# Two of the six modulation rows of a feed-forward are summed on VectorE instead of TensorE

## Chip, core and metric

The program runs on one core of one Trainium2 chip. The metric is device time in microseconds (us) of one execution, given as the median of several runs. TensorE, VectorE (DVE), ScalarE (ACT), GpSimd (POOL) and the DMA queue of SyncE (SP) work side by side; each has its own list of instructions and takes them in that order.

## The reference, cut to what matters

Two blocks follow each other on 256 tokens of width 1024. The first (gated convolution, mLSTM, mixture of experts) is not touched. The second has two layers; all of it is float32:

```python
cond = silu(c)                                        # one row of 1024
for i in range(2):
    mod = (cond @ ada_w[i] + ada_b[i])[:, None, :]    # ada_w[i] is 1024 x 6144
    shift1, scale1, gate1, shift2, scale2, gate2 = split(mod, 6, axis=-1)
    h = rmsnorm(x, norm1_g[i]) * (1.0 + scale1) + shift1
    x = x + gate1 * attention_i(h)
    h = rmsnorm(x, norm2_g[i]) * (1.0 + scale2) + shift2
    x = x + gate2 * swiglu(h, f_w_in[i], f_w_out[i])
```

The change concerns `shift2` and `scale2` of layer 0 of this second block: a vector of 1024 against a matrix of 1024 x 1024, twice.

## The kernel before, in words

Large products are made from float32 operands split in a high and a low part (`split`, lines 92 to 109: ACT copies the high part, DVE subtracts it for the low part) and three matmuls for each pair (`mm3`, line 127). Weights come in pieces of 1 MB into eight buffers named `raw` (`load`, line 74), each load being one instruction in SP's list that waits until a buffer is free.

The modulation rows (`ada_steps`, line 187) are matmuls of a different kind: the conditioning column, repeated to 32 columns, is the stationary operand, and 512 columns of `ada_w` move. Four such matmuls go to four column groups of the array (output partitions 0, 32, 64, 96) into one PSUM bank. A step is one load of 1 MB and four matmuls; the bias is added by further matmuls of the same output shape from a 12-row tile (`bias`). The last step copies the bank out (`adarow`), and either turns it into columns (`ada_cols`, tile `adac`) or spreads it over all partitions (`ada_gate`, tile `adag`).

The steps are not run where they are needed. They stand in a Python list, `queue`, and `fill` (line 182) takes the next one at fixed places: after each of the twelve weight pieces of attention 0 (`dense`, steps "D"; tile `dense`), after each of its eight heads (`values`, steps "V") and after each piece of the feed-forward's first product (`first`; tiles `fg` and `fu`). Attention 0 so has 20 places. Before the change the list for layer 0 has 19 entries: `ada1` (gate1 and shift2, 8 loads and an end), `ada2` (scale2, 4 loads and an end), `ada3` (gate2, 4 loads and an end). The 9 entries of the next layer's `ada0` follow when feed-forward 0 begins. The list's order is the program's order; the framework then sets each engine's own order from it, so that steps move a little to either side.

In attention 0 the string at line 1287 is the order of the work. After three weight pieces come the transposes of queries and keys (`pT`, copied out by ACT into `T`), the scores of two heads (`sc`), softmax on DVE and ACT (`nm`, `ee`), then for each head four transposes of the weights (`wT`), a copy by ACT (`wTs`) and four matmuls with the values (`po`), then scores of the next two heads, and so on. Queries and keys are rotated by six small POOL operations a piece (`rope`, lines 1205 to 1210). The gap between attention 0 and feed-forward 0 holds the row norm (`nt` are its transposes).

Of the kernel before, what the change touches and what calls it, by code (L numbers as in the profile page):

```python
# [7 lines left out]
F32 = mybir.dt.float32  # L8
# [4 lines left out]
ALU = mybir.AluOpType  # L13
# [4 lines left out]
D = 1024  # L18
# [34 lines left out]
def kernel(ctx: ExitStack, tc: tile.TileContext, I, cst, out):  # L53
# [3 lines left out]
    const = ctx.enter_context(tc.tile_pool(name="const", bufs=1))  # L57
# [8 lines left out]
    def pb(name):  # L66
        return psum.tile([128, 512], F32, name=name, tag="pb", bufs=3)
# [14 lines left out]
    def load_k(w, k0, k, n0, n):  # L82
        return load(w[k0 * 128:(k0 + k) * 128, n0:n0 + n].rearrange("(k p) n -> p k n", p=128), k, n)
# [49 lines left out]
    def mm(o, a, b, first=True, last=True):  # L133
        chain["mm"] = PE.matmul(o, a, b, start=first, stop=last, skip_group_check=True)  # L134
        return chain["mm"]
# [51 lines left out]
    def ada_steps(key, w, ccol, b0, nb, use):  # L187


        st = {}  # L190
        g = 4 // nb
        n = KT // g

        def step(i):
            def f():
                if i == 0:
                    st["ps"] = pc("ada")
                ps = st["ps"]
                if g == 1:
                    wt = load(w[i * 128:(i + 1) * 128, b0 * 512:(b0 + 4) * 512].rearrange("p (k n) -> p k n", k=4), 4, 512)  # L200
                else:
                    wt = load_k(w, g * i, g, b0 * 512, nb * 512)
                if i == 1:
                    for b in range(nb):
                        mm(ps[32 * g * b:32 * g * b + 32, :], sel12[:, b0 + b, :], bias_t[key], False, False)
                for k in range(g):
                    for b in range(nb):
                        j = g * b + k
                        kt = g * i + k
                        mm(ps[32 * j:32 * j + 32, :], ccol[:, kt:kt + 1].to_broadcast([128, 32]),  # L210
                           wt[:, b, :] if g == 1 else wt[:, k, b * 512:(b + 1) * 512], i == 0, i == n - 1)
            return f

        def end():
            a = pools["work"].tile([128, 512], F32, name="adarow", **pools.get("adarow", {}))
            ACT.copy(a, st["ps"])
            use(a)

        return [step(i) for i in range(n)] + [end]

    def ada_cols(a, nb=4):
        cols = pb("adac")[:, :4 * nb].rearrange("p (j b) -> p j b", b=4)
        for b in range(4):
            mm(cols[:, :, b], a[:, b * 128:(b + 1) * 128], selc[:, 0:4] if nb == 4 else selc[:, 4:6])
        return cols
# [41 lines left out]
    def ada1(key, w, ccol):  # L267
        def use(a):
            mod["gate1"] = ada_gate(a, 4, "gate1")
            mod["sh2"] = copy_cols(ada_cols(a)[:, 2:4], f"sh2_{key}")  # L270

        return ada_steps(key, w, ccol, 4, 4, use)

    def ada2(key, w, ccol, g2):
        def use(a):
            mod["AB2"] = mod_cols(mod["sh2"].rearrange("p (j b) -> p j b", b=4), ada_cols(a, 2), g2(), f"AB2_{key}")

        return ada_steps(key, w, ccol, 8, 2, use)

    def ada3(key, w, ccol):  # L280
        def use(a):
            mod["gate2"] = ada_gate(a, 2, "gate2")

        return ada_steps(key, w, ccol, 10, 2, use)

    ssq = {}

# [47 lines left out]
    def norm_post(banks, AB, dve=lambda ks, ts: ks.start and ts.start, then=lambda n: None):  # L335
        Hh, Hl = new_h()
        for n, (ks, ts, d) in enumerate(modulated(banks, AB, lambda ks, ts: pools["work"].tile([128, 512], F32, name="gtmp", bufs=2)
                                   .rearrange("p (f t) -> p f t", f=4), dve)):
            DVE.tensor_copy(Hh[:, ks, ts], d)  # L339
            chain["H"] = sub_lo(Hl[:, ks, ts], d, Hh[:, ks, ts]).ins  # L340
            then(n)
        return Hh, Hl
# [1051 lines left out]
                SP.dma_start(out=out[0, t * 128:(t + 1) * 128, cols], in_=u[t][:, cols])  # L1394

    for i in range(2):
        queue += ada1(1 + i, w_ada2[i], cc2) + ada2(1 + i, w_ada2[i], cc2, lambda: n2c[i]) + ada3(1 + i, w_ada2[i], cc2)
        (layer0, layer1)[i](mod["AB1"])
        fill(len(queue) - 5)
        if i == 0:  # L1400
            queue += ada0(2, w_ada2[1], cc2, lambda: n1c[1])
        with tc.tile_pool(name=f"ffn{i}", bufs=1) as pp, tc.tile_pool(name=f"hif{i}", bufs=4) as hif:
            pools["hi"], pools["m"] = [hif]*4+[hib]*2, 0
            H = norm_post(nt, mod["AB2"])
            if i == 1:
                fg = act.tile([128, D], F32, name="fg", tag="gate1")
                SP.dma_start(out=fg, in_=I["final_g_2"].unsqueeze(0).to_broadcast([128, D]))
                u = [pp.tile([128, D], F32, name=f"u{t}") for t in range(2)]
            ffn(H, I["f_w_in_2"][i], I["f_w_out_2"][i], pp, finish if i == 1 else None)
        pools["hi"] = [hib]  # L1410
        fill(len(queue))
# [114 lines left out]
```

## Time and profile before

| | |
|---|---|
| median of 3 runs | 1429.44 us (1424.09 to 1435.59) |
| profiled execution | 1432.25 us, span of its instructions 1430.4 us |
| mean granted TensorE clock | 0.969 of full |
| busy: TensorE, DVE, ACT, POOL | 1291.1, 621.5, 489.2, 57.1 us |
| attention 0 (second block) | about 751 to 900 us of the span |
| feed-forward 0 | about 911 to 1110 us |

The profile is of one execution. Busy time is the union of an engine's instructions; shares are of the span. One float32 matmul leaves two records, so "x8" is four matmuls. In the list of waits and in the timelines, the bracket at a row's end is the idle time before it and who ended it.

### The profile page before, as it was taken

The page shows a single profiled execution, that of the slowest core. Times are in us where ns is not written, and L with a number is a line of the kernel's source. Part 1 is how long each engine was busy: PE and PEld are TensorE (multiplying, and loading weights), DVE is VectorE, ACT ScalarE, POOL GpSimd, SP SyncE. Part 2 cuts the span into 40 slices and gives each one's busy share as a digit, 9 for nine tenths or more (in the row PEclk, how much of TensorE's full clock was granted, in tenths as well). Part 3 has the DMA queues.
Part 4 walks back from the last instruction along what each step waited for, and adds up shares of the span by engine and source line. Part 5 has one row for each costly group of instructions (what it writes and reads, how often), then busy time and mean ns, then how long its engine had stood idle before and what let it go on. Part 6 is the DMA issues. An engine that isn't in the chain of part 4 may idle for free.

```text
span 1430.4 us, 20089 instructions
## 1 busy us (share of the span) xinstructions
PE 1291.1 (90%) x8152; PEld 888.9 (62%) x8152; DVE 621.5 (43%) x1076; ACT 489.2 (34%) x836; POOL 57.1 (4%) x98
## 2 busy tenths in 40 slices
PE   7999999999778887766669999999999999999997
PEld 2876869634223322131128777688999767799997
DVE  2897947521101111011046545744543764744554
ACT  3553444401000010010035545634443543644442
POOL 0000000000000000000003220000000120000000
PEclk9998999999999999998989999999999999999999
DMA  9966687799999999999997765767553765855500
GB/s 380 371 226 232 208 321 269 310 394 425 426 427 427 426 426 425 427 370 425 427 407 253 243 227 196 279 220 247 177 182 113 265 206 177 309 177 177 177 30 30
DMA packets 139161, 408.84 MB, mean 286 GB/s; under 512 B 6676, under 2 KB 86932, under 8 KB 108344
## 3 DMA queue, kind: packets, MB, share of 16 engines
q1 hardware_dynamic: 138488, 403.31, 74.1%
q10 hardware_dynamic: 576, 4.19, 0.7%
q8 instruction: 66, 1.08, 0.3%
q14 instruction: 31, 0.25, 0.0%
HBM read 406.43 MB, written 1.05 MB: 285 GB/s over the span
## 4 chain that ended last, share of the span: by engine, by line
PE 44%; DMA 6%; DVE 2%; ACT 1%; issue 1%; POOL 1%; SPq 0%; ACTq 0%; POOLq 0%; DVEq 0%
DMA raw<-experts_dram 5%; PE ada L134 3%; PE fu L129 3%; PE fg L130 3%; PE fg L129 3%; PE fg L131 3%; PE fu L130 3%; PE fu L131 3%; PE facc L129 3%; PE facc L130 3%; PE facc L131 3%; PE dense L129 2%; PE dense L130 2%; PE dense L131 2%; PE sc L134 1%
## 5 line engine op out<-in xcount | busy, mean ns | idle before, releaser
L102 DVE TENSOR_TENSOR lo<-raw,hi 128x1024 fp32r<-128x1024 f32 x120 | 145.0, 1228 | 128.6 <-ACT hi L100 125.6
L120 DVE TENSOR_TENSOR lo<-raw,hi 128x1024 fp32r<-128x1024 f32 x120 | 146.6, 1224 | 94.1 <-ACT hi L118 94.0
L100 ACT ACTIVATE hi<-raw 128x1024 fp32r<-128x1024 f32 x120 | 124.9, 1060 | 152.1 <-PE facc L131 79.1
L118 ACT ACTIVATE hi<-raw 128x1024 fp32r<-128x1024 f32 x120 | 126.2, 1058 | 125.2 <-issue 59.0
L134 PE MATMUL pu<-raw,xg 128*32 128x512 f32 (+1 forms) x512 | 112.1, 650 | 32.9 <-DMA raw<-experts_dram 32.9
L134 PE MATMUL pd<-raw,hT 128*32 128x512 f32 (+1 forms) x512 | 109.8, 609 | 17.7 <-DMA raw<-experts_dram 10.8
L134 PE MATMUL pg<-raw,xg 128*32 128x512 f32 (+1 forms) x512 | 105.7, 632 | 13.5 <-DMA raw<-experts_dram 12.5
L965 DVE TENSOR_TENSOR hid<-hid,pu 128x256 f32<-128x256 f32 x20 | 7.5, 418 | 230.2 <-PE pu L134 230.2
L134 PE MATMUL ada<-raw,cc 128*32 128x512 f32 x576 | 96.4, 633 | 9.1 <-DMA raw<-in_w_ada_dram 9.0
L129 PE MATMUL fg<-Hh,lo 128*128 128x256 f32 x352 | 100.5, 286 | 4.3 <-DVE Hh L339 4.3
L130 PE MATMUL fg<-Hl,hi 128*128 128x256 f32 x352 | 100.5, 286 | 0.9 <-DVE Hl L125 0.9
L129 PE MATMUL fu<-Hh,lo 128*128 128x256 f32 x352 | 100.8, 286 | 0.0
L131 PE MATMUL fg<-Hh,hi 128*128 128x256 f32 x352 | 100.3, 285 | 0.0
L130 PE MATMUL fu<-Hl,hi 128*128 128x256 f32 x352 | 100.1, 284 | 0.0
L131 PE MATMUL fu<-Hh,hi 128*128 128x256 f32 x352 | 100.0, 284 | 0.0
L134 PEld LDWEIGHTS pu<-raw,xg 128*32 128x32 f32 (+1 forms) x512 | 28.2, 125 | 102.3 <-DMA raw<-experts_dram 56.2
L134 PEld LDWEIGHTS pd<-raw,hT 128*32 128x32 f32 (+1 forms) x512 | 30.3, 117 | 85.3 <-issue 57.3
L129 PE MATMUL dense<-hi,Hl 128*128 128x256 f32 x288 | 82.9, 288 | 0.5 <-DVE Hl L125 0.5
L130 PE MATMUL dense<-lo,Hh 128*128 128x256 f32 x288 | 81.6, 284 | 0.0
L131 PE MATMUL dense<-hi,Hh 128*128 128x256 f32 x288 | 81.4, 284 | 0.0
L1005 ACT ACTIVATE yh<-pd 128x512 fp32r<-128x512 f32 x20 | 11.9, 597 | 180.3 <-DVE pd L1003 180.3
L129 PEld LDWEIGHTS fg<-Hh,lo 128*128 128x128 f32 x352 | 68.0, 193 | 6.4 <-issue 4.7
(406 smaller groups left out, 2633.8 us busy)
## 6 DMA issues: line engine op xcount, KB each, us to landing
raw<-experts_dram SPq DMA_DIRECT2D x188, 1024.0 KB, 19.5
raw<-in_ada_w_dram SPq DMA_DIRECT2D x48, 1024.0 KB, 6.5
raw<-in_f_w_in_dram SPq DMA_DIRECT2D x44, 1024.0 KB, 5.0
raw<-in_w_ada_dram SPq DMA_DIRECT2D x24, 1024.0 KB, 6.2
raw<-in_f_w_out_dram SPq DMA_DIRECT2D x22, 1024.0 KB, 5.5
raw<-in_w_in_dram SPq DMA_DIRECT2D x20, 1024.0 KB, 9.9
raw<-in_a_w_qkv_dram SPq DMA_DIRECT2D x12, 1024.0 KB, 10.1
raw<-in_b_w_qkv_dram SPq DMA_DIRECT2D x6, 1024.0 KB, 4.8
```

Of the source, the lines that this page charges most:

```text
L100: ACT.activation(hv, src, AF.Copy)
L102: DVE.tensor_tensor(lv, src, hv.bitcast(F32), ALU.subtract)
L118: ACT.activation(hv, src, AF.Copy)
L120: DVE.tensor_tensor(lv, src, hv.bitcast(F32), ALU.subtract)
L129: PE.matmul(o, al, bh, start=first, stop=False, skip_group_check=True)
L130: PE.matmul(o, ah, bl, start=False, stop=False, skip_group_check=True)
L131: PE.matmul(o, ah, bh, start=False, stop=last, skip_group_check=True)
L134: chain["mm"] = PE.matmul(o, a, b, start=first, stop=last, skip_group_check=True)
L965: DVE.tensor_tensor(hid[:, c], hid[:, c], pgu[1][:, c], ALU.mult)
L1005: ACT.activation(yh, pd, AF.Copy)
```

## The change

For layer 0 alone, `ada1` and `ada2` give way to three lists: `ada_gate1` (gate1 alone, 4 loads and an end), and `sum_shift` and `sum_scale`, six entries each. Such a sum clears a 128 x 1024 tile (`adasum`, in one of the two buffers of the row norm) on POOL, loads the bias row into its first partition by a DMA of its own, and then lets DVE multiply each 128 x 1024 slice of the weights by the conditioning column and add it in place, two instructions a load, eight a sum. Its last entry collapses the 128 partitions by eight matmuls with one moving column of ones (`sum_cols`), and one DVE instruction puts the result into the columns that the norm uses. The next load is asked for one entry ahead of its use. The list is now 22 entries long. gate1 and gate2 stay as matmuls; layer 1 is as before.

```diff
+    def sums(key, part, use):
+        st = {"w": []}
+        def load_one(i):
+            st["w"].append(load_k(I["ada_w_2"][key - 1], 2 * i, 2, part * D, D))
+        def begin():
+            st["a"] = pools["xn"].tile([128, D], F32, name="adasum", tag=pools["xn_tag"])
+            POOL.memset(st["a"], 0.0)
+            SP.dma_start(out=st["a"][0:1, :], in_=I["ada_b_2"][key - 1:key, part * D:(part + 1) * D])
+            load_one(0)
+        def add(i):
+            def f():
+                if i < 3:
+                    load_one(i + 1)
+                wt = st["w"].pop(0)
+                for k in range(2):
+                    DVE.scalar_tensor_tensor(st["a"], wt[:, k, :], cc2[:, 2 * i + k:2 * i + k + 1], st["a"],
+                                             op0=ALU.mult, op1=ALU.add)
+            return f
+        return [begin] + [add(i) for i in range(4)] + [lambda: use(st["a"])]
+    def sum_cols(a):
+        cols = pb("adac")[:, 0:8]
+        for j in range(8):
+            mm(cols[:, j:j + 1], a[:, j * 128:(j + 1) * 128], ones[:, 0:1])
+        return cols
...
-        queue += ada1(1 + i, w_ada2[i], cc2) + ada2(1 + i, w_ada2[i], cc2, lambda: n2c[i]) + ada3(1 + i, w_ada2[i], cc2)
+        key = 1 + i
+        if i == 0:
+            mod_tile("AB2", key)
+            queue += ada_gate1(key, w_ada2[i], cc2) + sum_shift(key, 3, "AB2") + sum_scale(key, 4, n2c[i], "AB2")
+        else:
+            queue += ada1(key, w_ada2[i], cc2) + ada2(key, w_ada2[i], cc2, lambda: n2c[i])
+        queue += ada3(key, w_ada2[i], cc2)
```

What the engines' lists show. First TensorE at the second pair of heads of attention 0, before (`ada` rows are the modulation matmuls):

```order
L1163 MATMUL pT<-cs,tok_5688 128x128 x4
L134 MATMUL ada<-bias,cs 32x512
L1261 MATMUL wT<-cs,ee 128x128 x4
L134 MATMUL ada<-bias,cs 32x512
L134 MATMUL ada<-raw,cc_89 32x512
L134 MATMUL po<-tok_5763,wTs 128x128 x4
L134 MATMUL ada<-raw,cc_89 32x512 x3
L1261 MATMUL wT<-cs,ee 128x128 x4
L134 MATMUL ada<-raw,cc_89 32x512
L134 MATMUL po<-tok_5763,wTs 128x128 x4
L134 MATMUL ada<-raw,cc_89 32x512 x3
L134 MATMUL sc<-T_5781,T_5774 128x256 x8
```

and the same place now:

```order
L1197 MATMUL oT<-cs,o 128x128 x4
L1228 MATMUL pT<-cs,tok_5601 128x128 x4
L1228 MATMUL pT<-cs,tok_5673 128x128 x4
L1326 MATMUL wT<-cs,ee 128x128 x4
L134 MATMUL sc<-T_5761,T_5754 128x256 x4
L134 MATMUL po<-tok_5743,wTs 128x128 x4
L134 MATMUL adac<-ones,adasum 128x1 x8
L1326 MATMUL wT<-cs,ee 128x128 x4
```

The modulation matmuls that stood between `wT` and `po` are gone; half of the next scores and the eight matmuls of `sum_cols` stand there now, and six matmuls of the next weight piece, then the second `po` and the other scores, follow.

Second, TensorE from the end of attention 0 to the first product of feed-forward 0, before:

```order
L131 MATMUL oacc<-hi,oTh 128x512
L134 MATMUL ada<-raw,cc_89 32x512 x4
L134 MATMUL ada<-bias,cs 32x512 x4
L134 MATMUL ada<-raw,cc_89 32x512
L317 MATMUL nt<-cs,xn 128x128 x8
L134 MATMUL ada<-raw,cc_89 32x512 x11
L317 MATMUL nt<-cs,xn 128x128 x8
L129 MATMUL fg<-Hh,lo 128x256
```

now:

```order
L130 MATMUL oacc<-lo,oTh 128x512
L131 MATMUL oacc<-hi,oTh 128x512
L134 MATMUL ada<-raw,cc_89 32x512 x4
L382 MATMUL nt<-cs,xn 128x128 x16
L129 MATMUL fg<-Hh,lo 128x256
L130 MATMUL fg<-Hl,hi 128x256
```

and, inside feed-forward 0 where its second group of columns begins, now:

```order
L130 MATMUL fu<-Hl,hi 128x256
L131 MATMUL fu<-Hh,hi 128x256
L134 MATMUL adag<-gtmp,selrr 128x512 x4
L134 MATMUL ada<-bias,cs 32x512 x3
L134 MATMUL ada<-raw,cc_89 32x512
L129 MATMUL fg<-Hh,lo 128x256
```

Of the 32 modulation matmuls and 4 of bias for layer 1, 16 and all 4 of bias stood in the gap; now the gap holds the last four of gate2, and all 36 of layer 1 stand inside the feed-forward, in six rows of four and in the pieces 1, 3 with 1 of bias, 3 of bias with 1, and 3.

Third, DVE at the first scores of attention 0, before (`lo` are the low parts of weights, `nm` to `ee` the softmax):

```order
L102 TENSOR_TENSOR lo<-raw,hi 128x1024 x6
L1241 TENSOR_REDUCE nm<-sc 128x2 x2
L1242 TENSOR_SCALAR nm<-nm 128x4
L1241 TENSOR_REDUCE nm<-sc 128x2 x2
L1242 TENSOR_SCALAR nm<-nm 128x4
L1249 RECIPROCAL rr<-es 128x4
L1250 SCALAR_TENSOR_TENSOR rq<-rr,nlam,es 128x2
L1252 SCALAR_TENSOR_TENSOR ee<-ee,rq 128x256 x2
```

now:

```order
L306 SCALAR_TENSOR_TENSOR adasum<-raw,cc_89,adasum 128x1024 x2
L102 TENSOR_TENSOR lo<-raw,hi 128x1024 x2
L306 SCALAR_TENSOR_TENSOR adasum<-raw,cc_89,adasum 128x1024
L1306 TENSOR_REDUCE nm<-sc 128x2 x2
L125 TENSOR_TENSOR gtmp<-adarow,gtmp 128x512
L1307 TENSOR_SCALAR nm<-nm 128x4
L1306 TENSOR_REDUCE nm<-sc 128x2 x2
L306 SCALAR_TENSOR_TENSOR adasum<-raw,cc_89,adasum 128x1024
L1307 TENSOR_SCALAR nm<-nm 128x4
L306 SCALAR_TENSOR_TENSOR adasum<-raw,cc_89,adasum 128x1024
L1314 RECIPROCAL rr<-es 128x4
L306 SCALAR_TENSOR_TENSOR adasum<-raw,cc_89,adasum 128x1024
```

The first six of the sixteen additions stand between the low parts and the softmax steps of the first two heads; the other ten follow among those of the next two, the last two of them just ahead of the first `oTl`.

## Rows read from the trace of the kernel before

**Rows 1.** The page, part 1 (busy us, share, instructions) and part 4 (chain).
```profile
PE 1291.1 (90%) x8152; PEld 888.9 (62%) x8152; DVE 621.5 (43%) x1076; ACT 489.2 (34%) x836; POOL 57.1 (4%) x98
...
PE 44%; DMA 6%; DVE 2%; ACT 1%; issue 1%; POOL 1%; SPq 0%; ACTq 0%; POOLq 0%; DVEq 0%
```
**Rows 2.** Stretches: length, busy PE, PEld, DVE, ACT, POOL, granted clock, DMA share, GB/s.
```profile
767.00:818.00 51.00, 51.00 (x391) 41.90 (x391) 26.42 (x54) 28.88 (x67) 14.54 (x30) 1.00 0.71 242
930.00:950.00 20.00, 19.99 (x130) 18.18 (x130) 9.39 (x9) 7.25 (x8) 0.00 (x0) 1.00 0.57 201
...
911.00:914.00 3.00, 2.55 (x12) 2.48 (x12) 3.00 (x6) 2.87 (x4) 0.00 (x0) 0.50 1.01 378
```
**Rows 3.** Stretches, tile ada alone: length, busy PE, PEld, ACT, clock, DMA.
```profile
751.00:900.00 149.00, 25.84 (x124) 3.86 (x128) 1.84 (x3) 1.00 0.66 227
910.00:1110.00 200.00, 6.02 (x40) 0.91 (x40) 0.57 (x1) 0.99 0.58 199
```
**Rows 4.** The same view, tile adac alone (busy PE, PEld, DVE).
```profile
751.00:900.00 149.00, 2.01 (x16) 1.95 (x16) 0.33 (x2) 1.00 0.66 227
```
**Rows 5.** The same view, tile adag alone (busy PE, PEld, ACT).
```profile
751.00:900.00 149.00, 1.47 (x8) 0.60 (x8) 2.14 (x4) 1.00 0.66 227
```
**Rows 6.** Chain of waits in attention 0: start us, us, what.
```profile
787.58 0.99 PE ada L134 x6
788.57 1.02 PE pT L1163 x8
789.59 0.44 PE wT L1261 x4
790.03 1.83 PE ada L134 x10
791.86 1.09 PE po L134 x8
...
821.27 0.97 PE ada L134 x2
...
863.61 1.93 PE sc L134 x16
```
**Rows 7.** Timeline of TensorE, norms before attention 0 and before feed-forward 0: start, us, what.
```profile
744.39 1.97 PE L317 MATMUL nt<-cs,xn 128*128 128x128 f32 x8 [5.49 <-ACT xn L310]
...
904.12 2.77 PE L134 MATMUL ada<-raw,cc 128*32 128x512 f32 x22
907.47 1.09 PE L317 MATMUL nt<-cs,xn 128*128 128x128 f32 x8 [0.57 <-DVE xn L312]
```
**Rows 8.** Timeline of ACT in attention 0.
```profile
789.19 1.07 ACT L1164 COPY T<-pT 128x512 f32<-128x512 f32 x2
790.15 0.60 ACT L1264 COPY wTs<-wT 128x512 f32<-128x512 f32 x1
...
812.01 1.07 ACT L239 COPY gate<-adag 128x512 f32<-128x512 f32 x2
```
**Rows 9.** DVE groups, shapes apart: line, operation, count | busy us, mean ns | idle before.
```profile
L102 DVE TENSOR_TENSOR lo<-raw,hi 128x1024 fp32r<-128x1024 f32 x120 | 145.0, 1228 | 128.6 <-ACT hi L100 125.6 <-PE oT L1132 1.4 <-PE pT L1163 1.3
L626 DVE SCALAR_TENSOR_TENSOR uacc<-upad,pk,uacc 128x256 f32<-128x256 f32 x120 | 52.1, 483 | 0.4
...
L965 DVE TENSOR_TENSOR hid<-hid,pu 128x256 f32<-128x256 f32 x20 | 7.5, 418 | 230.2 <-PE pu L134 230.2
```
**Rows 10.** Timeline of DVE in attention 0.
```profile
782.97 2.48 DVE L102 TENSOR_TENSOR lo<-raw,hi 128x1024 fp32r<-128x1024 f32 x2
...
793.79 0.16 DVE L1274 TENSOR_TENSOR oss<-oss,rr 128x2 f32<-128x2 f32 x1 [3.37 <-ACT jk L1273]
```
**Rows 11.** Timeline of POOL, before attention 0 and in it.
```profile
747.25 0.54 POOL L297 TENSOR_TENSOR rstd<-ms,half 128x1 f32<-128x1 f32 x1 [1.37 <-DVE ms L1078]
...
784.33 1.30 POOL L1206 TENSOR_TENSOR rope<-tok,rot 128x64 f32<-128x64 f32 x1
785.59 0.32 POOL L1207 TENSOR_TENSOR rope<-tok,rot 128x64 f32<-128x64 f32 x1
```

More of the change, by code (lines that the diff above doesn't have):

```diff
@@ L284, in ada3, with sum_gate, use, mod_tile @@
         return ada_steps(key, w, ccol, 10, 2, use)
+    def sums(key, part, use):
[22 more added lines that the diff above has]
+        return cols
+    def sum_gate(key, part, name):
+        def use(a):
+            g = act.tile([128, D], F32, name=name)
+            for j in range(2):
+                ps = pb("adag")
+                mm(ps, ones, a[:, j * 512:(j + 1) * 512])
+                ACT.copy(g[:, j * 512:(j + 1) * 512], ps)
+            mod[name] = g
+        return sums(key, part, use)
+    def mod_tile(name, key):
+        mod[name, key] = const.tile([128, 2, 8], F32, name=f"{name}_{key}")
+    def sum_shift(key, part, name):
+        return sums(key, part, lambda a: DVE.tensor_copy(mod[name, key][:, 1], sum_cols(a)))
+    def sum_scale(key, part, gcol, name):
+        return sums(key, part, lambda a: DVE.scalar_tensor_tensor(mod[name, key][:, 0], sum_cols(a), 1.0, gcol,
+                                                                  op0=ALU.add, op1=ALU.mult))
+    def ada_shift(key, part, w, ccol, name):
+        return ada_steps(key, w, ccol, 2 * part, 2, lambda a: DVE.tensor_copy(
+            mod[name, key][:, 1].rearrange("p (j b) -> p j b", b=4), ada_cols(a, 2)))
+    def ada_gate1(key, w, ccol):
+        def use(a):
+            mod["gate1"] = ada_gate(a, 2, "gate1")
+        return ada_steps(key, w, ccol, 4, 2, use)
     ssq = {}
@@ L1403 @@
             pools["hi"], pools["m"] = [hif]*4+[hib]*2, 0
-            H = norm_post(nt, mod["AB2"])
+            H = norm_post(nt, mod.get(("AB2", key)) or mod["AB2"])
             if i == 1:
```

## The prediction

> **What bounds the kernel now.** I read the page first: TensorE is busy 90% of the span, DVE 43%, and 44% of the chain is TensorE's [rows 1]. A share over the whole program says little of attention 0, so the stretches came next. From 767 to 818 us, where the sums will be made, TensorE is busy all 51.0 us while DVE is busy 26.4 us; inside feed-forward 0, from 930 to 950 us, TensorE is busy 19.99 of 20 us [rows 2]. Third, the chain in attention 0 runs through TensorE and through the modulation matmuls themselves [rows 6]. So a microsecond taken off TensorE there is one off the end, as long as nothing else fills the hole; and one put into feed-forward 0 is paid in full. The gap between the two is the exception: its second set of transposes waits 0.57 us for DVE's normalised rows although 2.77 us of modulation matmuls have run meanwhile [rows 7]. TensorE's work there is free.
>
> **What leaves TensorE in attention 0.** Modulation matmuls go in passes: four that go to four column groups last about as long as one alone. Three (6 records) take 0.99 us, five take 1.83, and one alone (2 records) 0.97 [rows 6]. What counts is therefore the number of passes, not of matmuls. All of them from 751 to 900 us keep TensorE busy 25.84 us [rows 3], which is 25 passes at 0.97, or 24.3 us, the rest being overlapped ends and the first pass of the gap. Beside them stand two sets of `adac`, 2.0 us for 8 matmuls [rows 4], and two of `adag`, 1.5 us [rows 5]. Together 27.8 us.
>
> Now. Of gate1's four steps two are still ahead of the first weight piece; the others are split 1, 3 and 4: three passes. Three steps of gate2 stand in the last pair of heads as 1, 3, 1, 3, 1, 3 with one pass of bias: seven. Ten passes are 9.7 us. One `adag` remains there, 0.7 us. The sixteen matmuls of `sum_cols` have one moving column and a full 128 x 128 stationary part; the nearest rows are those of `adac` with 2 and 4 columns, 0.25 us each [rows 4], so 4.0 us (at least half of that, since the loads of their weights alone are busy almost as long in the same row; I take 4.0). Sum 14.4, so **13.4 us less on TensorE** in attention 0.
>
> **What comes back in feed-forward 0.** The list grew from 19 to 22 entries against 20 places, so gate2's last step and end move behind attention 0, and the next layer's 36 matmuls move behind these. Before, 20 of the 36 stood in the gap for nothing, and feed-forward 0 held 16 in five passes: 6.02 us busy in 40 records [rows 3], 4.9 us as steps of the chain. Now it holds all 36 as 1, 3+1, 3+1, 3 and six fours: ten passes, 9.7 us, and gate2's `adag`, 0.7. TensorE has no idle there [rows 2], so this costs **5.5 us**. Net of matmuls: -7.9 us.
>
> **What was hiding waits.** The removed passes were cover for copies on ACT. At the first pair of heads TensorE took 0.99 us of modulation, 1.02 of `pT`, 0.44 of `wT`, 1.83 of modulation, then `po` [rows 6]. Before `po` may start, ACT copies both `T` (1.07 us) and `wTs` (0.60, some 0.5 of it beyond the start of the next) [rows 8]. Now gate1's copies (1.07 us, same rows) stand ahead of these on ACT, and between `wT` and `po` only two score matmuls (eight take 1.93 us [rows 6]), which themselves need `T`. Counting from the end of `adag`: `pT` and `wT` are done at 1.5 us; ACT ends the gate's copies near 1.1, `T` at 2.2, `wTs` at 2.8. TensorE is idle 0.7 us before the scores and 0.1 before `po`; the second head's `wTs` is behind two reads of `po`, 0.6 us more. I get 1.5 us for the first pair and 1.0 for each of the next two, where six matmuls of `dense`, `sum_cols` or one pass of modulation stand as cover: 3.5 us. The last pair keeps its modulation matmuls.
>
> **What DVE takes on.** One addition has two float32 tensors and a column: the same operation over 256 columns, 120 of them back to back, takes 52.1/120 = 0.43 us of queue; over 1024 columns a two-tensor operation takes 1.23 us [rows 9]. I take 1.24 us, sixteen are 19.8 us. DVE has 24.6 us idle in the 51 us [rows 2], in pieces up to 3.4 us where it waits for ACT [rows 10]. Laying the new list over the old starts, the softmax of the first two heads is ready at about 782.6 and 784.9 us and wanted at 788; that of the next two is 1.5 to 3 us later than before, against some 6 us of slack; `lo` of the piece D12 comes 0.2 us late. So the additions themselves nearly fit. POOL suffers: a rotation step that meets `lo` takes 1.30 us and ends with it, and 0.32 us alone [rows 10, 11]. If an addition holds it alike, the rotation of D11 and D21, six steps each, ends up to 2 us after `pT` wants it; if not, nothing. I take 1.0 for both. Waits in attention 0: 3.5 + 0.2 + 1.0 = **4.7 us**, bounds 3 and 8.
>
> The Trainium skill, "Vector Engine (DVE) Microarchitecture Reference", section 7 "Points that are easy to get wrong", says that this operation halves its throughput when both tensors are non-bf16 and in SBUF, which is what an addition is. The rows do not agree: 483 ns over 256 columns with both in SBUF against 418 ns for a plain two-tensor operation of that width [rows 9], far from double. By the rule the sixteen would take 39 us instead of 19.8; it is a rival below.
>
> **The small things.** POOL clears two tiles ahead of its first rotation, after the last `rstd` at 747.8 us [rows 11]; the first rotation waits for the whole first product of `dense` anyway, so they hide. The first bias row's DMA waits for the first of them in SP's list, ahead of the tenth load: 1 to 2 us later, for data that DVE takes only behind the low parts of four weight pieces. The twelve loads stay 12 MB; their buffers come free by DVE instead of TensorE, a few us later, with a look-ahead of eight. 0, bounds 0 and 2. At the start of feed-forward 0, gate2's `adarow` copy, `gtmp` and its low part now stand on ACT and DVE, which were busy 2.87 and 3.00 of 3 us there [rows 2]: 0.5 us, bounds 0 and 1.3. And the gap: TensorE now has 3 us of work in it instead of 7. The clock stood at half (1.2 GHz) from 911 to 914 us [rows 2], behind transposes that had ended at 908.6 [rows 7]; if it falls earlier, the second eight transposes take 1.97 instead of 1.09 us [rows 7] and another 3 us of the first product run at half. 1.0 us, bounds 0 and 2.5.
>
> **Sum.** -13.4 + 5.5 + 4.7 + 0.5 + 1.0 = -1.7 us, so about 1430.5 against the profiled 1432.25; that execution is 2.8 us above the median of the runs, so 1427.7 us as a median. This is **no change** that can be told: 1% (14.3 us) is about what a measurement of this kernel resolves.
>
> **Rivals.**
> - *The holes fill* (chance 0.16). The framework has already moved scores and `dense` matmuls into the holes; if the copies are never late and POOL is not held, -7.9 us with at most 1.5 of waits: 1421 to 1423. For it: TensorE has no idle in the 51 us today [rows 2]. Against it: it had modulation matmuls to run in those places.
> - *DVE's queue becomes the bound: slower* (0.18). Between 767 and 818 us 26.4 + 19.8 = 46.2 us must fit into 51 less the 7 us that TensorE gains there. Additions stand ahead of `nm`, `rr` and `rq` in the list, so each may put off a softmax by 1.2 us. It decides from 1.7 us of lateness at TensorE beyond my 4.7. If half of DVE's idle time cannot be used, 7.5 us of additions go on top: 1435; if none can, 19.8 us: 1447.
> - *The halving rule holds* (0.03). 19.5 us more on DVE, about 10 of them beyond all idle: 1438.
> - *The work only moves* (part of the forecast): 5.5 of the 13.4 us reappear in feed-forward 0 for certain. A gain over 14.3 us would need every removed pass to pay and none to come back: 0.02.
>
> Forecast, -6 to +3 us about 1427.7: 0.61. The range leaves out the rare ends: low 1420.5 (all holes filled, and a run of the faster kind), high 1438 (the DVE rival's nearer end). Faster by over 1%: 0.02. Slower by over 1%: 0.04, the far end of the DVE rival. Within: 0.94.
>
> **What would show it.** Modulation matmuls in attention 0 busy about 10.5 us instead of 25.8, and in feed-forward 0 about 10.8 instead of 6.0; sixteen `adasum` additions of 1.2 us (2.4 would give the rule right), done before the second pair's `oTl`; attention 0 ending some 8 to 9 us earlier and feed-forward 0 some 2 us earlier than now; TensorE idle before `po` and `sc`, released by ACT's `T` and `wTs`, not by DVE. I am wrong if those waits name `ee` or `nm`, or if rotation steps of POOL end with additions and `pT` waits for them by more than 2 us.

## The result and the profile after

The changed kernel takes **1440.2 us** (median of 20 runs) beside 1430.4 us for the kernel before: 1.0081 of it, 95% interval 1.0062 to 1.0100. The forecast was 1427.7 us and no change; the range to 1438 doesn't hold the time. The ratio is taken over all runs, so it can differ a little from the quotient of the two medians. The profiled execution has a span of 1438.7 us.

Both profiles by stage, in us: the experts (first `pg` to last `acc`), attention 0 (first `dense` to last `oacc`), the gap, feed-forward 0. The pairs of heads are numbered 0 to 3, each from its transposes `pT` on. "At half" is, within the three later pairs (764 to 890 us), the sum of length times (1 - granted clock), an estimate of what the lower clock costs there.

| profile | experts | attention 0 | of it at half | gap | feed-forward 0 |
|---|---|---|---|---|---|
| before | 456.4 | 149.0 | 0.0 | 10.7 | 197.8 |
| after | 461.9 | 149.5 | 6.8 | 10.8 | 206.9 |
| forecast for after | as before | 140.3 | 0 | as before | 204.8 |

Three stages lost 5.5, 9.2 and 2.1 us against the forecast. The spans differ by only 8.3 us because a stage ahead of the experts, the same in both programs, was 6.5 us longer in the profile of before.

The page of after, part 1, answers [rows 1]; its first number is TensorE's busy time, with the sums gone from it no smaller than before:

```profile
PE 1293.8 (90%) x8096; PEld 893.5 (62%) x8096; DVE 640.9 (45%) x1091; ACT 488.8 (34%) x835; POOL 68.3 (5%) x100
```

Stretches of after, columns as in [rows 2]: the experts' middle, the place of the sums, pair 2, the gap, feed-forward 0.

```profile
320.00:700.00 380.00, 294.77 (x1523) 99.92 (x1523) 40.31 (x89) 31.12 (x62) 0.00 (x0) 0.94 1.00 415
...
767.00:818.00 51.00, 48.16 (x369) 42.29 (x367) 46.18 (x69) 31.79 (x72) 23.56 (x28) 1.00 0.90 310
818.00:830.00 12.00, 12.00 (x47) 10.79 (x48) 3.89 (x10) 2.65 (x7) 0.71 (x1) 0.50 0.52 190
903.00:917.00 14.00, 9.73 (x35) 6.78 (x36) 11.55 (x21) 11.16 (x23) 0.56 (x1) 0.51 0.48 157
930.00:950.00 20.00, 20.00 (x137) 16.79 (x132) 8.77 (x9) 8.32 (x11) 0.00 (x0) 1.00 0.58 194
```

The same view of before, for the stretch of the experts, of which the prediction has no row, and for the stretch of pair 2:

```profile
320.00:700.00 380.00, 293.76 (x1547) 101.67 (x1542) 42.44 (x96) 31.18 (x62) 0.00 (x0) 0.95 1.00 421
...
818.00:830.00 12.00, 12.00 (x71) 5.67 (x70) 4.38 (x9) 5.94 (x15) 0.71 (x1) 1.00 0.84 276
```

Read the DMA columns of the experts: the share is 1.00 in both, so DMA sets this stage's end; it moves 421 GB/s in the one and 415 in the other. In the place of the sums DVE's 46.18 us are the 46.2 of the prediction, and TensorE lacks 2.8 of its 51 us. Pair 2 runs at 0.50, which is 1.2 of 2.4 GHz; before it ran at 1.00.

Stretches of after for single tiles: `ada` in attention 0 and in feed-forward 0 (answers [rows 3]), then `adac` in attention 0 ([rows 4]), then `adag` in both ([rows 5]). TensorE's busy time is the second number.

```profile
751.00:900.00 149.00, 10.65 (x48) 1.60 (x52) 0.59 (x1) 0.95 0.65 222
910.00:1118.00 208.00, 13.42 (x72) 1.83 (x72) 1.16 (x2) 0.98 0.58 198
...
751.00:900.00 149.00, 5.26 (x32) 5.40 (x32) 0.33 (x2) 0.95 0.65 222
...
751.00:900.00 149.00, 0.74 (x4) 0.30 (x4) 1.07 (x2) 0.95 0.65 222
910.00:1118.00 208.00, 0.74 (x4) 0.30 (x4) 1.05 (x2) 0.98 0.58 198
```

The additions of after (count, ns shortest/median/longest, first and last start), the answer to [rows 9]:

```profile
L306 DVE SCALAR_TENSOR_TENSOR adasum<-raw,cc,adasum x16: 1278/1285/1343, 766.8 to 813.8; 128x1024 f32<-128x1024 f32 x16
```

POOL of after beside these additions, a rotation of pair 2 ([rows 11] has 0.32 us for a step alone):

```profile
809.01 1.19 POOL L1270 TENSOR_TENSOR rope<-tok,rot 128x64 f32<-128x64 f32 x1 [1.21 <-ACT tok L1280]
810.16 1.30 POOL L1271 TENSOR_TENSOR rope<-tok,rot 128x64 f32<-128x64 f32 x1
...
815.27 1.29 POOL L1275 TENSOR_TENSOR tok<-rope 128x64 f32<-128x64 f32 x1
```

TensorE of after: scores of pair 1, then pair 2, then the start of feed-forward 0:

```profile
794.12 1.13 PE L134 MATMUL sc<-T,T 64*128 64x256 f32 x4
...
813.78 0.60 PE L1197 MATMUL oT<-cs,o 128*128 128x128 f32 x4
814.22 0.60 PE L1228 MATMUL pT<-cs,tok 128*128 128x128 f32 x4
816.62 0.66 PE L1228 MATMUL pT<-cs,tok 128*128 128x128 f32 x4 [1.80 <-POOL tok L1275]
817.11 0.60 PE L1326 MATMUL wT<-cs,ee 128*128 128x128 f32 x4
817.95 3.78 PE L134 MATMUL sc<-T,T 64*128 64x256 f32 x8 [0.24 <-ACT T L1229]
821.66 2.07 PE L134 MATMUL po<-tok,wTs 128*128 128x128 f32 x8
823.52 3.41 PE L134 MATMUL adac<-ones,adasum 128*128 128x1 f32 x16
...
914.12 1.92 PE L134 MATMUL ada<-raw,cc 128*32 128x512 f32 x2
918.24 1.06 PE L134 MATMUL ada<-raw,cc 128*32 128x512 f32 x6
919.23 1.04 PE L134 MATMUL ada<-bias,cs 12*32 12x512 f32 x2
```

Where modulation passes stood between transposes and `po` in [rows 6], TensorE now has only transposes, scores and one-column matmuls. It waits 1.80 us for the held rotation, then the clock falls, and `po` takes 2.07 us where [rows 6] has 1.09.

### The profile page after: what moved, and what is told of

It is laid out like the page before. It is cut to its first block, busy times and chain, and to the rows that moved or that the text cites. A ratio compares the mean times of both kernels' runs of the same rounds, so it can differ in the third digit from the quotient of the medians.

```text
span 1438.7 us, 20006 instructions
## 1 busy us (share of the span) xinstructions
PE 1293.8 (90%) x8096; PEld 893.5 (62%) x8096; DVE 640.9 (45%) x1091; ACT 488.8 (34%) x835; POOL 68.3 (5%) x100
## 4 chain that ended last, share of the span: by engine, by line
PE 42%; DMA 7%; DVE 3%; ACT 2%; issue 2%; POOL 1%; SPq 0%; POOLq 0%; DVEq 0%; ACTq 0%
DMA raw<-experts_dram 6%; PE fu L129 3%; PE fg L130 3%; PE fg L129 3%; PE fg L131 3%; PE fu L130 3%; PE fu L131 3%; PE facc L129 3%; PE facc L130 3%; PE facc L131 3%; PE ada L134 3%; PE dense L129 2%; PE dense L130 2%; PE dense L131 2%; PE sc L134 2%
## 5 line engine op out<-in xcount | busy, mean ns | idle before, releaser
L102 DVE TENSOR_TENSOR lo<-raw,hi 128x1024 fp32r<-128x1024 f32 x120 | 145.7, 1231 | 125.7 <-ACT hi L100 125.6
L134 PE MATMUL pd<-raw,hT 128*32 128x512 f32 (+1 forms) x512 | 113.8, 613 | 17.9 <-DMA raw<-experts_dram 11.0
L134 PE MATMUL ada<-raw,cc 128*32 128x512 f32 x512 | 83.8, 623 | 10.2 <-DMA raw<-in_w_ada_dram 10.2
## 6 DMA issues: line engine op xcount, KB each, us to landing
raw<-experts_dram SPq DMA_DIRECT2D x188, 1024.0 KB, 19.8
```

The lines of the kernel that those rows point to most:

```text
L102: DVE.tensor_tensor(lv, src, hv.bitcast(F32), ALU.subtract)
```

## The experiments

Each kernel was timed beside the kernel before, and a ratio is always to that. The table at the end of the section has every profile's stages.

**Scores.** In after a head's two score tiles come from different PSUM buffers (`pa` and `pb`) and are ready at different times, so their matmuls (64 rows of the array each, upper or lower half) run in twos of one half. First, twos put into the kernel before:

```diff
-                    for t in range(2):
-                        for c in range(2):
+                    for c in range(2):
+                        for t in range(2):
```

> The kernel before, with the two loops around the score matmuls of attention 0 swapped, so that two matmuls on the same 64 rows of the array follow each other instead of alternating between the two halves. Nothing else moves. Theory (two 64-row matmuls in different halves run at the same time): eight score matmuls go from 1.93 us to 4 x 1.06 = 4.24 us in pairs 0, 2 and 3 and half of pair 1, 3.5 x 2.3 = +8 us, 1438.5 us or 1.0057 of the kernel before. Rival (a score matmul costs 0.24 us wherever it stands, as the prediction counted): 1430.4 us, no change. In between would mean that part of it hides beside waits.

Measured: 1.0003 (0.9983 to 1.0024). The edit missed its aim: it puts twos of alternating halves next to each other, and these cost hardly more than single ones in turn. Eight matmuls (16 records) on TensorE of this kernel, where [rows 6] has 1.93:

```profile
773.94 2.10 PE L134 MATMUL sc<-T,T 64*128 64x256 f32 x16
```

The changed kernel with both tiles from `pa`, so that the halves alternate:

```diff
-                    pc = [pa("sc"), pb("sc")]
+                    pc = [pa("sc"), pa("sc")]
```

> The changed kernel, but both score tiles of a head come from the same four PSUM buffers, so that neither half of a head's four score matmuls is ready long before the other and the halves alternate again. Theory (the lost pairing costs 4 to 5 us in attention 0): attention 0 from 149.4 to 144.5 to 146 us if the 13.65 us at half clock stay, the whole 1435 to 1436 us. The order around the scores moves too (the transposed outputs come later), which can make new waits of 1 to 2 us. Rival (scores cost the same in any order): 1440 us, or above by the new waits.

Measured: 1.0078 (1.0059 to 1.0097), attention 0 148.5 us. Two score matmuls of a head (4 records) on its TensorE:

```profile
795.48 0.70 PE L134 MATMUL sc<-T,T 64*128 64x256 f32 x4 [0.29 <-ACT T L1229]
```

They take 0.70 us; two of one half take 1.13 in the timeline of after. All score matmuls are busy 11.4 us here, 16.9 in after and 9.1 before; part of the 16.9 is at half clock. The time did not follow: 8.5 us are at half here and new waits for `ee` (2.3 us) and `o` (1.0) came with the new order. So the price is shown, and the gain from paying it back is not.

**Rotation.** The changed kernel with four POOL instructions for a rotation instead of six:

```diff
+            ct = pp.tile([128, 2, 2, 2, 8], F32, name="ct")
+            for m, b in enumerate((cosb, sinb)):
+                for a in range(2):
+                    ACT.copy(ct[:, m, :, a, :], b)
...
-                POOL.tensor_tensor(r[:, 0], x1, c, ALU.mult)
...
+                for m in range(2):
+                    POOL.tensor_tensor(r[:, m], v[:, :, :, 0:16], ct[:, m].rearrange("p t a d -> p t (a d)")[:, :, None, :]
+                                       .to_broadcast([128, 2, 4, 16]), ALU.mult)
```

> The changed kernel, with the rotation of queries and keys in attention 0 done by four GpSimd instructions instead of six (cosine and sine doubled once into a small table). TensorE's order is that of the changed kernel. Theory (GpSimd's instructions wait one by one behind VectorE's two-tensor instructions, so six of them take 7.6 us and the transposes of pair 2 come 1.8 us late, and this wait sets off 13.65 us at half clock): the rotation of pair 2's keys ends 2.6 us sooner, the transposes wait for nothing, no stretch at half clock stands between 816 and 832 us, 1431 to 1433 us, 0.994 of the changed kernel. Rival 1 (VectorE's full queue is the bound): the transposes are on time but values and softmax come as late as before, 1439 to 1440 us. Rival 2 (the clock falls for the sparse transposes and small matmuls between the dense stretches, not for the wait): the half-clock stretch stays, and only the 1.8 us come back, 1438.4 us.

Measured: 1.0078 (1.0054 to 1.0103), attention 0 146.3 us. Its stretches in pairs 2 and 3:

```profile
818.00:830.00 12.00, 12.00 (x91) 10.88 (x90) 7.36 (x27) 6.35 (x26) 1.41 (x2) 1.00 0.53 204
850.00:862.00 12.00, 12.00 (x54) 10.57 (x55) 5.98 (x22) 4.46 (x20) 0.70 (x1) 0.57 0.09 38
```

The wait is gone, and half clock has left pair 2 (1.00) for pair 3 (0.57). So the fall does not need the wait. The theory that the wait sets it off is refuted.

**Additions without missing cover, and missing cover without additions.** First the changed kernel with additions of 8 columns, which leaves the sums incomplete:

```diff
-                    DVE.scalar_tensor_tensor(st["a"], wt[:, k, :], cc2[:, 2 * i + k:2 * i + k + 1], st["a"],
+                    DVE.scalar_tensor_tensor(st["a"][:, 0:8], wt[:, k, 0:8], cc2[:, 2 * i + k:2 * i + k + 1], st["a"][:, 0:8],
```

> The changed kernel, but each of the 16 additions covers 8 of its 1024 columns (the sums of shift and scale are left incomplete; loads, order and passes stay). Theory 1 (what costs is TensorE's missing cover: with the passes gone the stretches between the dense parts hold only transposes, 64-row scores and one-column matmuls, and the clock falls in one of them): the 1.8 us wait for GpSimd's rotation goes, but a stretch of 8 to 17 us at half clock stays in attention 0 and the scores stay in twos; attention 0 146 to 148 us, the whole 1436 to 1438 us. Theory 2 (the additions themselves cost it, by filling VectorE and holding GpSimd): attention 0 139 to 142 us without a stretch at half clock, the whole 1430 to 1432 us.

Measured: 1.0065 (1.0042 to 1.0087), attention 0 145.3 us, which is 4.2 less than in after; in it 3.4 at half in pair 3:

```profile
858.00:868.00 10.00, 10.00 (x51) 8.92 (x51) 5.36 (x21) 4.29 (x20) 0.70 (x1) 0.66 0.09 36
```

Then all passes kept, the additions beside them:

```diff
+                if key == 1 and b0 in (4, 8):
...
+                    for k in range(g):
+                        a = st["a"].rearrange("p (b n) -> p b n", b=2)
+                        v = wt[:, 2:4, :] if g == 1 else wt[:, k, :].rearrange("p (b n) -> p b n", b=2)
+                        DVE.scalar_tensor_tensor(a, v, ccol[:, g * i + k:g * i + k + 1], a, op0=ALU.mult, op1=ALU.add)
```

> The kernel before, with all its passes, and beside them the change's 16 additions of 128x1024 on VectorE from the same loaded rows, into a scratch tile that nothing reads: the additions alone, with TensorE's cover kept. Theory 1 (missing cover): GpSimd's rotation is held as in the changed kernel, but passes stand where TensorE would wait; attention 0 149 to 151 us, no stretch at half clock in it, the whole 1430 to 1432 us, within 0.2 % of the kernel before. Theory 2 (the additions themselves cost it): attention 0 154 us or more, the whole 1435 us or more.

Measured: 1.0049 (1.0029 to 1.0069); attention 0 153.6 us, none of it at half in the three later pairs. Both theories had a part: additions cost 4.6 us of themselves here, where they begin earlier than in after, 3.0 of it one wait for POOL in pair 0, where no pass stands. The wait, then the stretch of the later pairs:

```profile
769.52 0.66 PE L1171 MATMUL pT<-cs,tok 128*128 128x128 f32 x4 [2.97 <-POOL tok L1218]
...
764.00:890.00 126.00, 123.02 (x849) 92.70 (x848) 76.40 (x148) 67.53 (x160) 30.41 (x50) 1.00 0.65 220
```

But the clock stays up even behind that longer wait when passes follow, and falls with hardly any addition when they are gone.

**Filler passes.** The changed kernel with four passes that nobody reads, in heads 2 to 5:

```diff
+                    if h in (2, 3, 4, 5):
+                        extra = psum.tile([128, 512], F32, tag='pc', name="extra")
+                        for _ in range(1):
+                            for b in range(4):
+                                mm(extra[32 * b:32 * b + 32, :], cc2[:, b:b + 1].to_broadcast([128, 32]), H[0].bitcast(F32).rearrange("p k t -> p (k t)")[:, 512 * b:512 * b + 512])
```

> The changed kernel with four passes of four 32-column matmuls put back as pure filler, one in each of the heads of pairs 1 and 2 (before the transposes of its weights; their result is read by nobody, the output is not touched). So far a stretch at half clock stood in attention 0 of all seven kernels that run the sums on VectorE, and none in the two that keep the passes. Theory 1 (the missing passes let the clock fall): no more than 1.7 us lost to half clock in attention 0 (6.8 in the changed kernel), the fillers cost 4 x 0.98 = 3.9 us of which 2 us fall into waits; 1435 to 1437 us, faster than the changed kernel in spite of the added work. Theory 2 (the fall has another cause): the loss stays at 4 to 8 us and the kernel is 2 to 4 us slower than the changed kernel, 1442 to 1444 us.

Measured: 1.0085 (1.0054 to 1.0116). The mechanism came out, the time did not: attention 0 took 147.7 us with four more passes, 1.8 less than in after, and pair 2 stood at full clock, with a wait of 1.4 us for POOL still in it; but the whole was no faster than the changed kernel.

```profile
812.00:836.00 24.00, 22.47 (x158) 17.74 (x157) 15.06 (x32) 11.37 (x33) 8.32 (x9) 1.00 0.59 212
```

**Feed-forward 0.** The list emptied ahead of it:

```diff
-        fill(len(queue) - 5)
+        fill(len(queue) - (5 if i else 0))
```

> The changed kernel, but all that is left in the list is issued before the first feed-forward, so that layer 1's vector (ada0 of block 2) comes two places earlier, back to where the kernel before had it: its first passes beside the norm. Theory (the feed-forward's 9.1 us more are the moved passes, its gate's passes and the half clock at its start): feed-forward 0 from 207.7 back to 199 to 201 us, the stretch at half clock around the gap from 13.65 us back to about 3.4 us, the whole 1431 to 1433 us, 0.995 of the changed kernel. Rival (the feed-forward is longer for another reason, loads or VectorE): 1438 to 1440 us, feed-forward 0 still above 205 us. The passes must still be run somewhere: if the gap between attention and feed-forward grows by more than 3 us, half of the gain goes back there.

Measured: 1.0041 (1.0017 to 1.0064); feed-forward 0 196.8 us, the gap 14.3. And the list packed into 20 entries for 20 places:

```diff
-        return [begin] + [add(i) for i in range(4)] + [lambda: use(st["a"])]
+        def last():
+            add(3)()
+            use(st["a"])
+
+        return [begin] + [add(i) for i in range(3)] + [last]
```

> The changed kernel with the packed list alone (20 entries for 20 places). It is what the prediction assumed with a full list: feed-forward 0 and the gap as in the kernel before (197 to 198 and 10.7 us), attention 0 as in the changed kernel plus one pass and the gate, 147 to 150 us, with scores in twos and the rotation held. If the moved passes were the whole of feed-forward 0's 9.1 us, the whole is 1430 to 1433 us; if the feed-forward stays above 203 us, they were not.

Measured: 1.0021 (1.0003 to 1.0038); feed-forward 0 197.8 us, the gap 10.7, both as before. So the two left-over entries were the whole of its 9.1 us. Yet attention 0, at 145.1, was 3.9 us shorter than before and the kernel was still not faster.

**Repairs together.** The list finished, both score tiles from `pa` ("one ring" in the table), four rotation steps; then the same with the gate's entries behind the sums; then the packed list with one ring and four steps. Their diffs are those above, and for the second:

```diff
-            queue += ada_gate1(key, w_ada2[i], cc2) + sum_shift(key, 3, "AB2") + sum_scale(key, 4, n2c[i], "AB2")
+            queue += sum_shift(key, 3, "AB2") + sum_scale(key, 4, n2c[i], "AB2") + ada_gate1(key, w_ada2[i], cc2)
```

> The changed kernel with the three repairs together: the list finished before the first feed-forward, both score tiles from one set of buffers, the rotation in four instructions. If they add up (feed-forward and gap together 6.5 us less, rotation 3 us, scores 4 us): 1426 to 1428 us, 0.997 to 0.999 of the kernel before. If the clock falls in attention 0 for the missing cover whatever is repaired (4 to 8 us lost there in all four kernels looked at so far): 1430 to 1432 us, the same as the kernel before.

> As the kernel with three repairs, but the list has the two sums first and the gate of the attention behind them, so that the gates' passes stand in pairs 2 and 3, beside their transposes and scores, and the additions begin in pair 0. Missing cover: less than 3.4 us is lost to half clock in attention 0, and the kernel is 3 to 6 us faster than with the three repairs alone, 1422 to 1427 us. Rival (cover doesn't matter, the additions do): the same time as with the three repairs, or longer, since the additions now fall beside the rotation of pair 1.

> The changed kernel, but the last addition of each sum and its use share one entry of the list, so that the list has 20 entries for the 20 places of attention 0 and nothing of it is left for the first feed-forward or the gap; with it both score tiles from one set of buffers and the rotation in four instructions. The gap goes from 15.6 us (the kernel with three repairs) to about 10.8, feed-forward 0 stays at 197 to 198, attention 0 takes the one pass and the gate's matmuls that the gap held: 144 to 147 us. The whole 1425 to 1428 us, 0.996 to 0.999 of the kernel before, if the clock falls for no longer than in the kernel with three repairs (4.4 us lost); 1421 to 1424 us if the passes that now stand in pairs 2 and 3 keep the clock up.

Measured: 1.0001 (0.9985 to 1.0018), 1.0113 (1.0086 to 1.0139) and 1.0030 (1.0013 to 1.0046). With the gate last, attention 0 takes 160.1 us: additions begin in pair 0, the first transposes of pair 1 wait 3.7 us for POOL, a `dense` piece 4.1 us for `ee`, and 8.5 us are at half. To place passes as cover later while the sums come earlier was a bad trade. The control, four rotation steps in the kernel before:

> The kernel before with the rotation in four GpSimd instructions, all else and TensorE's order unchanged: whether this repair is worth something without the change. Both theories: nothing waits for GpSimd in attention 0 of the kernel before, so no change, 0.999 to 1.001 of it. If it is faster by more than 2 us, the repairs of the changed kernel owe that part to this edit and not to the sums.

Measured: 1.0009 (0.9993 to 1.0025): nothing. Two more, to see what kept the packed list from a gain (packed with four steps; the same with two filler passes in heads 4 and 5):

> The packed list (20 entries for 20 places) and the rotation in four GpSimd instructions, scores in twos as in the changed kernel. Attention 0 144 to 146 us with 2 to 5 us lost to half clock in pairs 1 to 3, feed-forward 0 198 us. If the clock is what takes the gain: 1428 to 1432 us, 0.999 to 1.001 of the kernel before, and the runs lose 3 to 6 us more to the clock than its runs (span times one less the granted clock). If something else takes it, the runs lose as much as those of the kernel before and the time is still not below it.

> The same with two filler passes of four 32-column matmuls (read by nobody) that stand in pairs 1 and 2 or behind pair 3: 2 us more of TensorE's work. If the clock takes the gain and cover keeps it: no half clock in pairs 1 to 3 where the fillers stand, attention 0 within 1 us of the kernel without fillers, the whole 1427 to 1431 us, equal to or below it. If not: 2 us above the kernel without fillers.

Measured: 1.0000 (0.9983 to 1.0017) and 1.0027 (1.0006 to 1.0049). The first has no half clock in pairs 1 to 3, an attention 0 that is 5.6 us shorter than before and all else equal around it, and is not faster. Its runs lose no more to the clock than those of the kernel before (span times one less the granted clock: medians 43.5 and 42.8 us), so by its expectation something other than the clock took the gain. The two filler passes only cost, 3.3 us of attention 0.

**The address.** Set beside each other, the profiles show it where nothing was changed: the experts take 461.1 to 463.8 us in all twelve kernels with the sums so far, 456.3 to 456.7 in the four that keep the old tiles. The change no longer makes the 32-byte tile `sh2_1`, which lay ahead of the buffers of loaded weights; in the built program these begin at byte 25568 of each partition, before at 25600. A trace holds no addresses; the next four kernels test it. The edit is one unused tile, of 8 columns (32 bytes) or 16:

```diff
+    const.tile([128, 8], F32, name="pad")
     rawp = ctx.enter_context(tc.tile_pool(name="raw", bufs=RAW_BUFS))
```

> The changed kernel with an unused 32-byte tile in front of the buffers of loaded weights, which puts them back to address 25600; no instruction changes. Theory (the address slows the expert weights' DMA from 426 to 420 GB/s): the expert stage 456 to 457 us instead of 462, the whole 5 to 6 us below the changed kernel, 1433 to 1435 us, 1.003 to 1.005 of the kernel before. Rival (something else of the change, or the runs' scatter): 461 to 463 us, 1439 to 1441 us.

> The kernel before with nothing but an unused 32-byte tile in front of the buffers, which moves them to 25632. Theory (an address that is 32 bytes off costs, whichever way): the expert stage 461 to 463 us, ratio 1.003 to 1.005. Rival: 456 to 457 us, ratio 1.000.

> The kernel before with an unused 64-byte tile in front of the buffers, which moves them to 25664, a multiple of 64 but not of 128. If what counts is a multiple of 64 bytes: the expert stage 456 to 457 us, ratio 1.000. If 128 or more is needed: 461 us or more, ratio 1.003 to 1.005.

> The packed list and the rotation in four (measured at 1.000 of the kernel before) with the buffers back at address 25600. Attention 0 143 to 146 us, gap and feed-forward as before, the expert stage 456 to 457 us: 4 to 6 us below the kernel before, 1423 to 1425 us, ratio 0.996 to 0.997. Rival (the address is not it): ratio 1.000.

Measured: the changed kernel with the old address 1.0012 (0.9989 to 1.0035), 1433.4 us; the kernel before moved by 32 bytes 1.0044 (1.0023 to 1.0065), by 64 bytes 1.0044 (1.0024 to 1.0064); the packed list with four steps and the old address **0.9960 (0.9938 to 0.9983)**, 1423.5 beside 1428.6 us. The experts' stretch of the changed kernel with the old address, then of the kernel before moved by 32 bytes:

```profile
320.00:700.00 380.00, 293.39 (x1560) 101.74 (x1560) 42.35 (x96) 30.98 (x62) 0.00 (x0) 0.96 1.00 421
```

```profile
320.00:700.00 380.00, 296.58 (x1529) 101.62 (x1527) 41.68 (x94) 31.12 (x62) 0.00 (x0) 0.93 1.00 415
```

The rate goes with the address: the two programs of each such comparison differ in nothing else. Loads of the experts in this stretch (count, KB, median us from issue to landing), before, after, and before moved by 32 bytes:

```profile
raw<-experts_dram SPq DMA_DIRECT2D x150, 1024.0 KB, 19.5
raw<-experts_dram SPq DMA_DIRECT2D x148, 1024.0 KB, 19.8
raw<-experts_dram SPq DMA_DIRECT2D x147, 1024.0 KB, 19.8
```

The version that beats both kernels, by its stretches (experts, attention 0, feed-forward 0):

```profile
320.00:700.00 380.00, 292.44 (x1548) 102.58 (x1542) 42.43 (x96) 31.19 (x62) 0.00 (x0) 0.96 1.00 420
752.00:895.00 143.00, 142.51 (x976) 119.47 (x980) 100.47 (x176) 77.58 (x176) 33.26 (x41) 0.99 0.68 237
907.00:1105.00 198.00, 197.91 (x1371) 180.05 (x1370) 95.43 (x97) 79.80 (x93) 0.54 (x1) 0.99 0.57 197
```

| profile of | experts | attention 0 | at half | gap | feed-forward 0 |
|---|---|---|---|---|---|
| before, swapped score loops | 456.3 | 149.3 | 0.0 | 10.7 | 199.2 |
| before + additions | 456.6 | 153.6 | 0.0 | 10.7 | 198.0 |
| before, four steps | 456.7 | 149.3 | 0.0 | 10.7 | 198.3 |
| before + 32 bytes | 462.6 | 150.1 | 0.0 | 10.7 | 199.1 |
| before + 64 bytes | 461.3 | 149.4 | 0.0 | 10.7 | 198.4 |
| after, list finished | 462.8 | 146.9 | 3.4 | 14.3 | 196.8 |
| after, one ring | 461.8 | 148.5 | 8.5 | 10.8 | 206.4 |
| after, four steps | 462.8 | 146.3 | 5.1 | 10.8 | 206.6 |
| after, 8 columns | 463.8 | 145.3 | 3.4 | 10.8 | 206.5 |
| after, fillers | 462.3 | 147.7 | 0.0 | 10.8 | 206.0 |
| after, three repairs | 461.1 | 143.6 | 1.7 | 15.6 | 196.8 |
| the same, gate last | 461.9 | 160.1 | 8.5 | 17.9 | 194.8 |
| after, packed | 462.4 | 145.1 | 1.7 | 10.7 | 197.8 |
| packed, one ring, four steps | 462.3 | 145.7 | 1.7 | 10.7 | 198.0 |
| packed, four steps | 462.5 | 143.4 | 0.0 | 10.7 | 197.1 |
| the same, fillers | 462.1 | 146.7 | 0.0 | 10.7 | 198.4 |
| after, old address | 456.3 | 146.8 | 3.4 | 10.8 | 206.5 |
| packed, four steps, old address | 456.8 | 143.0 | 0.0 | 10.7 | 198.2 |

## Why the prediction was wrong, point by point

- **The frame of the sum**, "-13.4 + 5.5 + 4.7 + 0.5 + 1.0" against the profiled time, and the step "The small things ... 0, bounds 0 and 2". It counted the tiles that the change adds and the loads' order, and not that a tile which it drops moves the buffers behind it. This is a term that the prediction put at nothing without asking for it: 5.5 us in the experts' stage, which ends before the first changed instruction starts. Putting the address back takes the ratio from 1.0081 to 1.0012; the forecast was 0.9988, just outside that interval (0.9989 to 1.0035). The fall of the ratio is worth more than 5.5 us, but the two intervals allow for that. Shown by four runs, in both directions. The rest of what the forecast missed lies in attention 0 (9.2 us, from the scores and the clock) and in feed-forward 0 (2.1), below.
- **What leaves TensorE**: right. 10.65 us of `ada` are left for 10.5 forecast, one `adag` of 0.74. A set of `adac` takes 1.84 us at full clock in the list-finished kernel, for 2.0 forecast.
- **"only two score matmuls (eight take 1.93 us)"**: mis-sized. I took 0.24 us a matmul from a row where the halves alternate. Two of one half take 1.13, and in the packed kernel with four steps, at full clock in the pairs, all scores are busy 15.5 us for 9.1 before: 6.4 us, for which the sum has no term. The tile `sc` alone, before and in that kernel:

```profile
751.00:905.00 154.00, 9.11 (x64) 6.51 (x64) 10.50 (x16) 15.12 (x64) 1.00 0.67 229
751.00:905.00 154.00, 15.48 (x64) 9.48 (x64) 10.82 (x16) 15.13 (x64) 0.99 0.69 241
```

- **No term for the clock in attention 0.** "1.0 clock" stood for the gap alone. The passes were not only cover for copies. In six profiles that keep them nothing is lost in the pairs; in the changed kernel's code 6.8, and 3.4 twice (list finished, old address). Fillers and the packed list (whose gate 2 passes move into pairs 2 and 3) bring it to 0 to 1.7. The timed runs point the same way: of the changed kernel's 20, the five at 1433 to 1436 us have a mean granted clock of 0.969 to 0.972, the five at 1450 to 1454 us one of 0.955 to 0.962. That missing matmuls let the clock fall is shown; which place it falls in varies between executions of the same instructions, and why is open.
- **Waits, 4.7 us**: a little over. TensorE idles 3.1 us in attention 0, 2.8 of it in the 51 us, released by POOL, by ACT's gate copies and by `T`, as named; not by `ee` or `nm`. POOL's hold, taken at 1.0, cost 1.8. With 1.6 us less of waits, 6.4 more of scores and 6.8 of clock, attention 0 should have missed by 11.6 us; it missed by 9.2, and no run shows where the other 2.4 went.
- **DVE**: right, 1.285 us an addition for 1.24. The Trainium skill, "Vector Engine (DVE) Microarchitecture Reference", section 7 "Points that are easy to get wrong", would have it at half throughput; the rows do not, 1.285 us beside 1.228 for a plain two-tensor operation of that size [rows 9]. (By its own figures that rival's "19.5 us more" is 39 - 19.8 = 19.2.) The rival "DVE's queue becomes the bound" gave the right sign for the wrong reason: most of what the additions cost of themselves comes through POOL (3.0 of 4.6 us in the kernel before with additions), and the time that it named was luck.
- **Feed-forward 0, +5.5 and 1.5 for its start**: mis-sized, 9.1 measured. The twelve passes there are 1, 3, bias 1, bias 3, 1, 3 and six fours: a bias matmul shares no pass with its neighbours (1.04 us of its own at 919.23, behind three others in 1.06), so two more than counted, and 1.4 us more are at half clock behind a gap that is now nearly without passes.

## What to carry to other kernels

Compare two traces stage by stage over the whole program, the stages without a changed instruction first: one that is bound by DMA shows a moved buffer, and a change that drops or adds a tile should be timed with its neighbours' addresses held. Price a matmul by a row with the same neighbours, and ask of passes that hide waits what the clock does when they are gone.

## What the runs showed of the hardware

- **Address and DMA rate.** 1 MB loads of 8 KB per partition land in a median of 19.5 us at an address of 25600 and 19.8 at 25568; at 25568, 25632 and 25664 alike the stage at 1.00 DMA share slows by 1.1 to 1.4% (461.3 to 462.6 us for 456.4). The Trainium skill, "DMA: Bandwidth & Descriptors", section "How a descriptor splits into AXI transactions", says that a descriptor whose start is no multiple of 256 bytes begins its first transaction at the 256-byte boundary below; for 8 KB we estimate from it 33 transactions in place of 32, 3% more. It writes of bytes that are fetched and does not say that this holds for the address that is written, as here. The runs agree in kind, with less than half of that in time; 25600 is the only one of the four that is such a multiple. It is also the only multiple of 128, so no run tells 256 from 128. By beats, which the page counts too, 25568 should cost more than 25632; the rows show 415 GB/s at both.
- **POOL beside additions.** A rotation step of 0.32 us takes 1.30 beside a two-tensor addition with a column, as beside `lo`. The Trainium skill, "Advanced Engine Details and Errata", section "GPSIMD Details", names the read and write interface that the two engines share, in conflict for two SBUF inputs; the rows agree.
